# Encoder block on one core: eight chunk pairs of the down projection as block products with weight sums made in DRAM

## The chip, the cores and the metric

The kernel runs on one core of one Trainium2 chip. The metric is the device time of one execution in microseconds (us); a comparison takes the median of several runs. The engines are PE (TensorE, matrix products), DVE (VectorE), ACT (ScalarE), POOL (GpSimd) and SP (SyncE, which issues most transfers). A transfer is carried out by the core's 16 DMA engines, whichever engine issued it.

## The reference

One encoder layer over 512 rows of 1024 columns, in float32: three parallel mixers, a gated feed-forward network (FFN) with 2816 hidden columns (22 tiles of 128), a final norm. The change is in the last product of the FFN, the down projection `act @ w_down`; what stands before it only matters for the order of the work.

```python
h = rms_norm(x, g);  z = h @ W_in                       # gates, latents, streams, memory queries
y = W_out( sum_b sigmoid(g_b) * (o_b @ W_branch_b) )    # attention, mLSTM, attention into memory
x = x + y
x = x + (silu(h2 @ w_gate) * (h2 @ w_up)) @ w_down      # h2 = rms_norm(x); 2816 hidden columns
out = rms_norm(x, g_final)
```

## The kernel before

Each float32 operand is split into a high and a low part, and a product of two 128-row tiles is three matmuls (`mm3`, L104 to L106: high by high, then the two mixed ones). `wload` loads a weight tile of 128x1024 (512 KB) from DRAM into `raw` (SP's queue, L94) and splits it: ACT makes `w_hi` (L85), DVE `w_lo` (L86). `raw` has two buffers and `w_hi`/`w_lo` three.

The code is written against a framework in which tiles have names, pools and buffer counts. A scheduler orders the instructions of each engine by their dependences and priorities; the written order is not the order on the chip. Each engine, SP and POOL among them, runs its own instructions strictly in order, so that an issue which waits holds all issues behind it on the same engine.

At the start SP loads the memory rows, the input and small constants, four tiles of `w_kt` (keys of the memory attention) and then the tiles of `w_zt`, the combined input projection. The z tiles are consumed by PE one after the other, some 6 us each, with attention work in between. POOL makes constants, norm roots, later a `memset` and small stores to `a_dr`.

The FFN uses 2x2 block products with seven multiplications for 19 of its 22 tiles. Its results `u` (tile f) go to `early` (f under 6, kept in SBUF as high and low parts) or to DRAM (`act_dr`, L951). The FFN's `th` and `u` are two-buffer tiles of the pool `fs`, which is released at its end; later pools lie on the same memory.

The down projection is `projection(...)` with `w_fd[half, c]`: two halves of 512 output columns, 11 chunk pairs c of two 128-row tiles each, four row tiles t. In the first half every chunk's activations are read back from `act_dr` and split (`act_load`), and 24 matmuls of 512 columns follow per chunk (4 row tiles, 2 tiles, 3 matmuls). In the second half row tile 3 is computed as two pieces of 256 columns, and the last three chunks are held in `wd_t` so that the row tiles finish one after the other. Then comes `add_part` (L877), the norm and the stores of the output.

Of the kernel before, what the change touches and what calls it, by code (L numbers as in the profile page):

```python
# [60 lines left out]
def block_kernel(ctx, tc, x, mem, pos, inv, g_mix, mem_g, g_ffn, g_final, g_q, g_kv, gate_bias,  # L61
# [966 lines left out]
    act_hi = fin.tile([P, NF - EARLY, S], F32R, name="act_hi")
    act_lo = fin.tile([P, NF - EARLY, S], F32R, name="act_lo")

    def act_side(c):
        if 2 * c < EARLY:
            return early[0], early[1], 2 * c
        return act_hi, act_lo, 2 * c - EARLY

    def act_load(c):
        for f in (2 * c, 2 * c + 1):
            if f >= EARLY:
                a = acte.tile([P, S], F32, name="act", tag="act", bufs=2)
                nc.sync.dma_start(out=a, in_=act_dr[f - EARLY])  # L1040
                split(act_hi[:, f - EARLY], act_lo[:, f - EARLY], a, scale=-0.5)
# [7 lines left out]
    def hold_down(lead):  # L1049
        return [wload(w_fd[1, c], into=wd_t[c - lead]) for c in range(lead, NF // 2)]  # L1050

    def gain_low(t):
        nc.gpsimd.tensor_tensor(out=xg[t][:, :H], in0=x2[t][:, :H], in1=gfin_b[:, :H], op=ALU.mult)

    def store(t, r):
# [1 line left out]
        A.activation(xg[t][:, :H], xg[t][:, :H], AF.Copy, scale=r)
        nc.scalar.dma_start(out=out[rows, :H], in_=xg[t][:, :H])
        n = H // 2 if t == NT - 1 else H
        for c0 in range(H, D, n):  # L1060
            cols = slice(c0, c0 + n)
# [86 lines left out]
```

## Time and profile before

| | us |
|---|---|
| median of three runs | 926.97 |
| lowest, highest | 925.7, 928.73 |
| the profiled execution | 925.3 |
| its span in the profile | 923.4 |
| PE busy | 905.1 |
| DVE busy | 636.1 |
| ACT busy | 509.2 |
| POOL busy | 85.2 |

The span is what the profiler saw of one execution; 1.9 us of that execution lie outside it. Busy times are sums over the whole span. Matmuls are pipelined: the time from one start to the next is the pace, and a row's mean of one is longer than it. DMA share is the mean busy share of the 16 DMA engines, and GB/s is what they moved.

### The profile page before, as it was taken

Reading aid. Unit: us, or ns where it says so; the run is one execution under the profiler, and the core shown is the slowest. Engines: PE = TensorE matmul, PEld = TensorE weight load, DVE = VectorE, ACT = ScalarE, POOL = GpSimd, SP = SyncE. Lnnn points to the kernel's source line nnn. Section 1 sums busy time; section 2 is a strip of 40 time slices with the busy share of each in tenths; the row PEclk is TensorE's granted clock in tenths of the full one; section 3 lists DMA queues with packets and bytes.
Section 4 is the critical chain, followed back from the end, with each engine's and each line's share of the span. In section 5 each row is a group of like instructions: output and inputs, shape, how many; then the busy total and the mean of one; then the engine's idle time right before and its main releaser. Section 6 shows DMA issues by size and latency. Waiting matters only on the chain.

```text
span 923.4 us, 13931 instructions
## 1 busy us (share of the span) xinstructions
PE 905.1 (98%) x5282; PEld 787.7 (85%) x5282; DVE 636.1 (69%) x1088; ACT 509.2 (55%) x896; POOL 85.2 (9%) x139
## 2 busy tenths in 40 slices
PE   7998999999999999999999999999999999999997
PEld 5987787878888788888888879999999999988886
DVE  5768968888684856677553855989898988354323
ACT  8565676686653456677574445545454545244222
POOL 2001002121111101001000500000000000000200
PEclk9999999999999999999999999999999999999999
DMA  7421244434432122121224250423434431365322
GB/s 274 161 75 47 77 133 125 157 121 140 140 111 92 50 86 83 40 87 60 78 69 160 90 191 17 160 93 125 149 115 127 159 115 69 105 225 162 106 76 91
DMA packets 36675, 104.82 MB, mean 114 GB/s; under 512 B 5169, under 2 KB 7537, under 8 KB 36609
## 3 DMA queue, kind: packets, MB, share of 16 engines
q1 hardware_dynamic: 34560, 99.65, 32.4%
q0 software_dynamic: 1184, 3.24, 1.0%
q10 hardware_dynamic: 864, 1.06, 0.3%
q8 instruction: 41, 0.67, 0.3%
q14 instruction: 26, 0.21, 0.1%
HBM read 97.55 MB, written 6.37 MB: 113 GB/s over the span
## 4 chain that ended last, share of the span: by engine, by line
PE 90%; DVE 4%; DMA 2%; ACT 1%; issue 1%; POOL 0%; POOLq 0%; DVEq 0%; SPq 0%; ACTq 0%
PE pg L104 17%; PE pg L106 17%; PE pg L105 17%; PE po L104 7%; PE po L106 7%; PE po L105 7%; PE psc L104 2%; PE psc L105 2%; PE psc L106 2%; PE ptp L818 2%; DVE w_lo L86 1%; PE ppv L588 1%; PE ppv L587 1%; DMA raw<-w_out_d 1%; PE ppv L586 1%
## 5 line engine op out<-in xcount | busy, mean ns | idle before, releaser
L86 DVE TENSOR_TENSOR w_lo<-raw,w_hi 128x1024 fp32r<-128x1024 f32 (+3 forms) x112 | 126.0, 1127 | 92.4 <-ACT w_hi L85 90.7
L104 PE MATMUL pg<-h_hi,w_hi 128*128 128x512 f32 (+1 forms) x476 | 175.2, 369 | 0.8 <-DVE q_lo L89 0.6
L105 PE MATMUL pg<-h_lo,w_hi 128*128 128x512 f32 (+1 forms) x476 | 175.6, 369 | 0.0
L106 PE MATMUL pg<-h_hi,w_lo 128*128 128x512 f32 (+1 forms) x476 | 175.1, 368 | 0.3 <-DVE w_lo L86 0.3
L85 ACT ACTIVATE w_hi<-raw 128x1024 fp32r<-128x1024 f32 (+3 forms) x112 | 107.0, 958 | 104.4 <-PE pg L105 57.2
L104 PEld LDWEIGHTS pg<-h_hi,w_hi 128*128 128x128 f32 x476 | 89.6, 188 | 15.4 <-DVE q_lo L89 0.8
L106 PEld LDWEIGHTS pg<-h_hi,w_lo 128*128 128x128 f32 x476 | 89.5, 188 | 14.8 <-DVE w_lo L86 0.7
L105 PEld LDWEIGHTS pg<-h_lo,w_hi 128*128 128x128 f32 x476 | 89.5, 188 | 13.7
L571 ACT ACTIVATE e<-e,ccol 128x512 f32<-128x512 f32 (+3 forms) x64 | 32.3, 554 | 28.2 <-DMA e<-a_dr 27.6
L1073 DVE TENSOR_REDUCE nm<-psc 128x1 f32<-128x512 f32 (+1 forms) x48 | 27.7, 596 | 19.9 <-PE psc L106 19.5
L576 DVE TENSOR_TENSOR e<-e,psc 128x512 f32<-128x512 f32 (+3 forms) x64 | 29.1, 482 | 17.5 <-POOL e L574 14.6
L1076 ACT ACTIVATE pn<-psc,nm 128x512 f32<-128x512 f32 (+1 forms) x48 | 29.4, 614 | 17.6 <-DVE nm L1073 17.6
L85 ACT ACTIVATE w_hi<-rawab 128x1024 fp32r<-128x1024 f32 x19 | 20.1, 1059 | 29.0 <-PE pg L105 17.4
L574 POOL TENSOR_SCALAR_AFFINE_SELECT e<-e 128x128 f32<-128x128 f32 x64 | 24.0, 384 | 121.5 <-ACT e L571 110.2
L104 PE MATMUL po<-h_hi,w_hi 128*128 128x256 f32 (+1 forms) x116 | 33.8, 291 | 1.4 <-ACT w_hi L85 1.4
L86 DVE TENSOR_TENSOR w_lo<-rawab,w_hi 128x1024 fp32r<-128x1024 f32 x19 | 23.2, 1222 | 16.1 <-ACT w_hi L85 16.0
L1079 ACT ACTIVATE pn<-pn,rs 128x512 f32<-128x512 f32 (+1 forms) x48 | 29.8, 651 | 7.7 <-DVE rs L1078 7.5
L105 PE MATMUL po<-h_lo,w_hi 128*128 128x256 f32 (+1 forms) x116 | 33.7, 290 | 0.0
L106 PE MATMUL po<-h_hi,w_lo 128*128 128x256 f32 (+1 forms) x116 | 33.6, 290 | 0.0
L86 DVE TENSOR_TENSOR s_lo<-e,s_hi 128x640 fp32r<-128x640 f32 x32 | 26.1, 825 | 4.3 <-ACT s_hi L85 2.6
L105 PE MATMUL po<-w_lo,act_hi 128*128 128x512 f32 (+1 forms) x74 | 27.4, 375 | 0.0
L85 ACT ACTIVATE w_hi<-s 128x1024 fp32r<-128x1024 f32 x19 | 20.1, 1059 | 12.9 <-PE pg L105 9.9
(511 smaller groups left out, 2565.3 us busy)
## 6 DMA issues: line engine op xcount, KB each, us to landing
raw<-w_zt_d SPq DMA_DIRECT2D x46, 512.0 KB, 3.4
raw<-w_fd_d SPq DMA_DIRECT2D x22, 512.0 KB, 3.4
e<-a_dr SPq DMA_DIRECT2D x32, 320.0 KB, 3.4
rawab<-w_fg_d SPq DMA_DIRECT2D x19, 512.0 KB, 3.8
rawab<-w_fu_d SPq DMA_DIRECT2D x19, 512.0 KB, 4.7
raw<-w_br_d SPq DMA_DIRECT2D x12, 512.0 KB, 3.5
raw<-w_out_d SPq DMA_DIRECT2D x8, 512.0 KB, 3.6
act_dr<-u SPq DMA_DIRECT2D x16, 256.0 KB, 3.9
```

What stands on the lines that cost most here:

```text
L85: A.activation(hi, src, AF.Copy)
L86: V.tensor_tensor(out=lo, in0=src, in1=hi, op=ALU.subtract)
L104: mm(ps, wh, ah, start=start and i == 0, stop=False, skip_group_check=more)
L105: mm(ps, wh, al, start=False, stop=False, skip_group_check=more)
L106: mm(ps, wl, ah, start=False, stop=stop and i == n - 1, skip_group_check=more)
L571: A.activation(e[:, c0:c0 + n], e[:, c0:c0 + n], AF.Exp, bias=ccol[:, j, d, row:row + 1])
L574: nc.gpsimd.affine_select(out=dg, in_=dg, pattern=[[sgn, P]], compare_op=ALU.is_ge, fill=0.0, base=0, channel_multiplier=-sgn)
L576: V.tensor_tensor(out=e[:, c0:c0 + n], in0=e[:, c0:c0 + n], in1=sc[:, t0:t0 + n], op=ALU.mult)
L818: nc.tensor.transpose(tp[:, c * 256 + q * P:c * 256 + (q + 1) * P], pn[q][:, (kt + c) * P:(kt + c + 1) * P], ident)
L1073: nc.vector.tensor_reduce(out=nm, in_=sc, axis=AX.X, op=ALU.max, negate=True)
L1076: nc.scalar.activation(pn, sc, AF.Exp, bias=nm, accum_out=sm)
L1079: nc.scalar.activation(pn, pn, AF.Copy, scale=rs)
```

## The change

Chunks 0 to 2 (the early tiles, C0 = 3) stay plain products. Chunks 3 to 10 (NC = 8) are computed as 2x2 blocks with seven products instead of eight. The blocks are: rows 0 to 255 and 256 to 511 of the activations, two tiles of the hidden columns per chunk, and two halves of the output columns. The three phases have two, three and two of the products per chunk; each uses some differences of activation blocks (`acts`, `lhs`) and some sums of weight blocks. The products accumulate in PSUM over the chunks, and `onto` adds or subtracts a finished bank to or from `x2`.

The sums of weight blocks (`t13`, `t24`) do not depend on the input of the layer but on `w_fd` alone. They are made in DRAM by `down_sums()`: SP copies a block from DRAM to DRAM (L843, L844, L851, L857 of the new code, 1 MiB each), and POOL issues transfers that add another block onto the copy (L847 2 MiB, L854 and L860 1 MiB; `accum_op=ALU.add`). Everything is done for two groups of four chunks. `beside` interleaves these steps with the units of the latent attention. `weights` takes its `raw` buffers from two pools in turn, `stage` and `fin`. At the very end the first half's weights of the plain chunks are loaded a second time (`ws`).

The diff, cut to its core:

```diff
+    t13, t24 = ([dram.tile([4, P, 2, 512], F32, name=f"{n}_{g}") for g in range(2)] for n in ("t13", "t24"))
...
+        def down_sums():
+            groups = range(2)
+            low, high = ([w_fd[u, C0 + 4 * g:C0 + 4 * g + 4] for g in groups] for u in range(2))
+            for g in groups:
+                nc.sync.dma_start(out=t13[g][:, :, 0], in_=low[g][:, :, 0:512])
+                nc.sync.dma_start(out=t13[g][:, :, 1], in_=high[g][:, :, 512:1024])
+                yield
+            for g in groups:
+                nc.gpsimd.dma_start(out=t13[g], in_=high[g][:, :, 0:512].unsqueeze(2).to_broadcast([4, P, 2, 512]),
+                                    accum_op=ALU.add)
+                yield
+            for g in groups:
+                nc.sync.dma_start(out=t24[g][:, :, 0], in_=t13[g][:, :, 0])
+                yield
+            for g in groups:
+                nc.gpsimd.dma_start(out=t24[g][:, :, 0], in_=high[g][:, :, 512:1024], accum_op=ALU.add)
+                yield
+            for g in groups:
+                nc.sync.dma_start(out=t24[g][:, :, 1], in_=t24[g][:, :, 0])
+                yield
+            for g in groups:
+                nc.gpsimd.dma_start(out=t24[g][:, :, 1], in_=low[g][:, :, 512:1024], accum_op=ALU.add)
+                yield
...
-        run(mla_units(oa_hi, oa_lo), fill, 0.9)
+        run(beside(mla_units(oa_hi, oa_lo), down_sums()), fill, 0.9)
...
+    def acts(c):
+        ab = (acte if c == 0 else fin).tile([P, 2, S], F32, name="ab", tag="ab", bufs=1 if c == 0 else 3)
+        for i in range(2):
+            nc.sync.dma_start(out=ab[:, i], in_=act_dr[2 * c + i])
...
+        d = fin.tile([P, 5, HS], F32, name="d", tag="d", bufs=NC)
+        V.tensor_tensor(out=d[:, 0], in0=a22, in1=a21, op=ALU.subtract)
+        V.tensor_tensor(out=d[:, 1], in0=a21, in1=a11, op=ALU.subtract)
+        V.tensor_tensor(out=d[:, 2], in0=d[:, 0], in1=a11, op=ALU.add)
+        V.tensor_tensor(out=d[:, 3], in0=a12, in1=d[:, 2], op=ALU.subtract)
+        nc.sync.dma_start(out=d[:, 4], in_=act_dr[2 * c + 1][:, HS:])
...
+        raw = (stage if raws[0] % 2 else fin).tile([P, 1024], F32, name="raw", tag="raw", bufs=2)[:, :n]
...
-    projection(((po,) * 4, (pg, pg, pt), (pt, po)),
-               w_fd, NF // 2, 3, act_side, hold_down, gain_low, store, last, act_load)
+    for c in range(C0):
+        w = weights(w_fd[0, c])
+        for t in range(2):
+            plain(py[t], t, c, w, c == 0, False)
+    for c in range(NC):
+        held[c] = acts(c)
+        w = weights(w_fd[0, C0 + c])
+        a = lhs(held[c][0][:, :, :HS], 2, "a2", -0.5)
+        block(px, a, 0, w, 0, c == 0, c == NC - 1)
+        block(py, a, 1, w, 512, False, c == NC - 1)
...
+    for c in range(NC):
+        w13 = weights(t13[g][i].rearrange("p i c -> p (i c)"))
+        s = lhs(held[c][1][:, 0:3], 3, "a3", 0.5)
+        block(pw, s, 0, w13, 0, c == 0, c == NC - 1)
+        block(pz, s, 1, w13, 512, c == 0, c == NC - 1)
+        w2 = weights(t24[g][i, :, 0])
+        block(px, s, 2, w2, 0, False, c == NC - 1)
...
+    for c in range(NC):
+        w = weights(w_fd[1, C0 + c][:, 512:1024], t24[g][i, :, 1])
+        a = lhs(held[c][1][:, 3:5], 2, "a2", -0.5)
+        block(pw, a, 0, w, 0, False, False)
+        block(pz, a, 1, w, 512, False, False)
```

SP's order at the start, before: behind the small constants come the loads of `w_kt` and `w_zt`, and nothing else.

```order
L265 DMA gh_94<-g_head_d 128x4
L265 DMA gq_t<-g_q_d 128x3
L265 DMA gkv_t<-g_kv_d 128x2
L94 DMA raw<-w_kt_d 128x1024 x4
L94 DMA raw<-w_zt_d 128x1024 x7
L94 DMA raw<-w_qk_d 128x256
```

Seven `w_zt` loads follow each other without anything between them; each waits for its `raw` buffer alone.

SP's order at the same place, after. `t_0_72` and `t_1_73` are the two groups of `t13`, `t_0_74` and `t_1_75` those of `t24`.

```order
L843 DMA t_0_72<-w_fd_d 512x512
L97 DMA raw<-w_kt_d 128x1024
L844 DMA t_0_72<-w_fd_d 512x512
L843 DMA t_1_73<-w_fd_d 512x512
L97 DMA raw<-w_kt_d 128x1024
L844 DMA t_1_73<-w_fd_d 512x512
L97 DMA raw<-w_kt_d 128x1024 x2
L97 DMA raw<-w_zt_d 128x1024
L851 DMA t_0_74<-t_0_72 512x512
L97 DMA raw<-w_zt_d 128x1024
L851 DMA t_1_75<-t_1_73 512x512
L97 DMA raw<-w_zt_d 128x1024 x3
L857 DMA t_0_74<-t_0_74 512x512
```

Six copies now stand ahead of the third `w_zt` load (the third to the fifth are the row with x3). Each L851 copy waits for the accumulating transfer of its group on POOL. Two more copies (L857, which wait for the L854 transfers) stand ahead of the sixth and the seventh `w_zt` load.

POOL's order behind the roots of the first norm, before:

```order
L115 TENSOR_TENSOR n_r<-n_v,mhalf 128x1 x6
L433 MEMSET t_633 32x512
L453 DMA a_dr<-brel 8x512
L453 DMA a_dr<-brel 8x384
L453 DMA a_dr<-brel 8x256
```

One `memset` and the first stores to `a_dr` follow. The same place after:

```order
L118 TENSOR_TENSOR n_r<-n_v,mhalf 128x1 x6
L847 DMA t_0_72<-w_fd_d 1024x1x512
L847 DMA t_1_73<-w_fd_d 1024x1x512
L436 MEMSET t_637 32x512
L854 DMA t_0_74<-w_fd_d 512x512
L854 DMA t_1_75<-w_fd_d 512x512
L860 DMA t_0_74<-w_fd_d 512x512
L860 DMA t_1_75<-w_fd_d 512x512
L456 DMA a_dr<-brel 8x512
```

The six accumulating transfers have come in between; each waits for the copies into its tile.

PE's order at the end of the FFN, before (with buffer numbers; `po_8600` is the FFN's last bank, `po_8684` to `po_8687` are the banks of the first half):

```order
L105 MATMUL po_8600<-h2t4l_5903,a22_hi_8520 128x256
L106 MATMUL po_8600<-h2t4h_5902,a22_lo_8521 128x256
L105 MATMUL po_8684<-w_lo_8751,early_h_5888 128x512
L106 MATMUL po_8684<-w_hi_8750,early_l_5889 128x512
L104 MATMUL po_8684<-w_hi_8750,early_h_5888 128x512
...
L104 MATMUL po_8687<-w_hi_8690,early_h_5888 128x512
...
L104 MATMUL po_8684<-w_hi_8788,act_hi_8667 128x512
```

Here 33 plain matmuls on `early` tiles stand between the FFN's last product and the first matmul on `act_hi`, and 39 of them stand ahead of that last product. After (`po_8618` is the FFN's last bank, `po_8702` and `po_8703` are `py`, `pg_8700` and `pg_8701` are `px`):

```order
L108 MATMUL po_8618<-h2t4l_5921,a22_hi_8538 128x256
L109 MATMUL po_8618<-h2t4h_5920,a22_lo_8539 128x256
L107 MATMUL po_8702<-w_hi_8724,early_h_5906 128x512
L107 MATMUL po_8703<-w_hi_8724,early_h_5906 128x512
L108 MATMUL po_8702<-w_lo_8725,early_h_5906 128x512
L109 MATMUL po_8702<-w_hi_8724,early_l_5907 128x512
L107 MATMUL po_8702<-w_hi_8724,early_h_5906 128x512
...
L107 MATMUL po_8702<-w_hi_8742,early_h_5906 128x512
L107 MATMUL po_8703<-w_hi_8742,early_h_5906 128x512
L107 MATMUL pg_8700<-w_hi_8769,a2h_8773 128x512
L107 MATMUL pg_8701<-w_hi_8769,a2h_8773 128x512
```

Of the plain matmuls of this phase 36 are left, and 12 of them stand ahead of the last product. The first weights behind it, `w_hi_8724`, are split from a `raw` buffer of the pool `fin`, which lies on the memory of the FFN's `th`; the `d` tiles lie on that of `u`.

## Rows read from the trace of the kernel before

**Rows 1.** The page's first line, busy times (us, share of the span, instructions) and chain that ended last.

```profile
span 923.4 us, 13931 instructions
PE 905.1 (98%) x5282; PEld 787.7 (85%) x5282; DVE 636.1 (69%) x1088; ACT 509.2 (55%) x896; POOL 85.2 (9%) x139
PE 90%; DVE 4%; DMA 2%; ACT 1%; issue 1%; POOL 0%; POOLq 0%; DVEq 0%; SPq 0%; ACTq 0%
```

**Rows 2.** Windows: start:end, length, busy us (count) by engine, PEclk, DMA share, GB/s.

```profile
0.00:10.00 10.00, 4.62 (x17) 3.19 (x17) 2.49 (x9) 5.43 (x11) 4.64 (x17) 1.00 0.80 283
10.00:20.00 10.00, 9.94 (x36) 7.83 (x37) 8.32 (x18) 10.00 (x18) 1.65 (x3) 1.00 0.96 343
20.00:30.00 10.00, 10.00 (x75) 9.27 (x74) 6.99 (x11) 7.92 (x12) 0.55 (x1) 1.00 0.39 121
```

**Rows 3.** Timeline of SP's queue: start, us, engine, line, operation, tiles, count.

```profile
15.08 9.80 SPq L94 DMA_DIRECT2D raw<-w_kt_d  x4
28.46 2.99 SPq L94 DMA_DIRECT2D raw<-w_zt_d  x2
34.34 3.02 SPq L94 DMA_DIRECT2D raw<-w_zt_d  x2
```

**Rows 4.** Timeline of PE at 12, 49 and 67 us.

```profile
12.37 0.63 PE L105 MATMUL psc<-w_lo,mt_hi 128*128 128x512 f32 x1
12.79 0.63 PE L106 MATMUL psc<-w_hi,mt_lo 128*128 128x512 f32 x1
14.30 0.39 PE L105 MATMUL psc<-w_lo,mt_hi 128*128 128x512 f32 x1
14.53 0.39 PE L106 MATMUL psc<-w_hi,mt_lo 128*128 128x512 f32 x1
48.99 0.39 PE L104 MATMUL ppv<-h_hi,w_hi 128*128 128x512 f32 x1
67.57 0.40 PE L105 MATMUL pg<-h_lo,w_hi 128*128 128x512 f32 x1
```

**Rows 5.** The page's DMA issues: tile, queue, count, KB each, us to landing.

```profile
raw<-w_zt_d SPq DMA_DIRECT2D x46, 512.0 KB, 3.4
```

**Rows 6.** Timeline of ACT: the splits that start consecutive chunks of the down projection.

```profile
828.81 1.06 ACT L85 ACTIVATE w_hi<-raw 128x1024 fp32r<-128x1024 f32 x1 [1.51 <-PE po L106]
834.25 1.06 ACT L85 ACTIVATE w_hi<-raw 128x1024 fp32r<-128x1024 f32 x1 [1.86 <-PE po L106]
867.07 1.06 ACT L85 ACTIVATE w_hi<-raw 128x1024 fp32r<-128x1024 f32 x1 [4.48 <-PE po L106]
872.61 1.06 ACT L85 ACTIVATE w_hi<-raw 128x1024 fp32r<-128x1024 f32 x1 [4.48 <-PE po L106]
```

**Rows 7.** Timeline of POOL: the first stores of `a_dr`.

```profile
73.54 1.31 POOL L453 DMA_DIRECT2D a_dr<-brel  x2 [29.55 <-DVE rs L1078]
```

**Rows 8.** Timeline of all engines where the FFN ends; releaser of idle time in brackets.

```profile
804.66 0.28 PE L106 MATMUL po<-h2t4h,a_lo 128*128 128x256 f32 x1
805.45 0.69 DVE L1013 TENSOR_TENSOR u<-th,u 128x512 f32<-128x512 f32 x1
806.16 0.33 SPq L951 DMA_DIRECT2D act_dr<-u  x1
808.58 1.15 ACT L88 ACTIVATE act_hi<-act 128x512 fp32r<-128x512 f32 x2 [4.64 <-DMA act_dr<-u]
```

**Rows 9.** Timeline of DVE: operations of 256, 512 and 1024 columns in a row.

```profile
750.36 0.42 DVE L994 SCALAR_TENSOR_TENSOR th<-th,g 128x256 f32<-128x256 f32 x1
750.70 0.69 DVE L1013 TENSOR_TENSOR u<-th,u 128x512 f32<-128x512 f32 x1
751.30 1.22 DVE L151 TENSOR_TENSOR s<-rawab 128x1024 f32<-128x1024 f32 x1
752.43 1.22 DVE L86 TENSOR_TENSOR s_lo<-rawab,s_hi 128x1024 fp32r<-128x1024 f32 x1
```

**Rows 10.** Timeline of DVE: the addition behind the last matmul.

```profile
917.21 0.42 DVE L877 TENSOR_TENSOR x<-po,x 128x256 f32<-128x256 f32 x1 [0.58 <-PE po L106]
```

More of the change, by code (lines that the diff above doesn't have):

```diff
@@ L38 @@
 EARLY = 6
+C0 = EARLY // 2
 NEG = -1.0e30
@@ L832, in mla_units, with beside @@
                             yield
+        def down_sums():
[21 more added lines that the diff above has]
+                yield
+        def beside(main, steps):
+            for _ in main:
+                next(steps, None)
+                yield
+            for _ in steps:
+                pass
         run(latent_units(), fill, 0.0)
@@ L1027, in block_kernel @@
     fin = ctx.enter_context(tc.tile_pool(name="fin", bufs=1))
[L1028 to L1041, printed above, removed]
     last = tc.alloc_tile_pool(name="last", bufs=1, side="right")
-    wd_t = [[last.tile([P, 1024], F32R, name=f"wd{c}{i}") for i in range(2)] for c in range(3)]
+    wd_t = [[last.tile([P, 1024], F32R, name=f"wd{c}{i}") for i in range(2)] for c in range(C0)]
     xg = [last.tile([P, D], F32, name=f"xg{t}") for t in range(NT)]
@@ L1047, in block_kernel @@
     bcast_rows(gfin_b, g_final)
[L1049 to L1055, printed above, removed]
-        rows = slice(t * P, (t + 1) * P)
[L1057 to L1061, printed above, removed]
+    NC = NF // 2 - C0
@@ new lines, in lhs, with weights @@
+    def lhs(src, n, tag, scale):
+        hi, lo = (fin.tile([P, n, HS], F32R, name=f"{tag}{i}", tag=f"{tag}{i}", bufs=2) for i in "hl")
+        split(hi, lo, src, scale=scale)
+        return hi, lo
+    raws = [0]
+    def weights(*srcs):
+        raws[0] += 1
+        n = 512 * sum(2 if src.shape[-1] == 1024 else 1 for src in srcs)
+        raw = (stage if raws[0] % 2 else fin).tile([P, 1024], F32, name="raw", tag="raw", bufs=2)[:, :n]
+        o = 0
+        for src in srcs:
+            w = src.shape[-1]
+            nc.sync.dma_start(out=raw[:, o:o + w], in_=src)
+            o += w
+        return wload(None, n=n, raw=raw)
@@ new lines, in block, with plain @@
+    def block(ps, a, i, w, o, first, last):
+        for t in range(2):
+            ts = slice(t * P, (t + 1) * P)
+            mm3(ps[t], [(a[0][:, i, ts], a[1][:, i, ts], w[0][:, o:o + 512], w[1][:, o:o + 512])],
+                start=first, stop=last, more=True)
+    def plain(ps, t, c, w, first, last, cols=slice(0, H)):
+        ts = slice(t * P, (t + 1) * P)
+        mm3(ps, [(early[0][:, 2 * c + k, ts], early[1][:, 2 * c + k, ts], w[0][:, k * H:(k + 1) * H][:, cols],
+                  w[1][:, k * H:(k + 1) * H][:, cols]) for k in range(2)], start=first, stop=last, more=True)
@@ new lines, in onto, with squares, gain @@
+    def onto(ps, t, c0, op=ALU.add, n=H):
+        xs = x2[t][:, c0:c0 + n]
+        V.tensor_tensor(out=xs, in0=xs, in1=ps, op=op)
+    def squares(t, c0, base_v, n=H):
+        junk = last.tile([P, H], F32, name="junk", tag="junk", bufs=2)[:, :n]
+        ss = keep.tile([P, 1], F32, name="ssx", tag="ssx", bufs=2 * NT)
+        A.activation(junk, x2[t][:, c0:c0 + n], AF.Square, accum_out=ss)
+        return partial(ss, base_v)
+    def gain(t, c0):
+        nc.gpsimd.tensor_tensor(out=xg[t][:, c0:c0 + H], in0=x2[t][:, c0:c0 + H], in1=gfin_b[:, c0:c0 + H], op=ALU.mult)
@@ L1062, in store @@
+    def store(t, v, c0, n):
+        r = keep.tile([P, 1], F32, name="f_r", tag="f_r", bufs=2)
+        nc.gpsimd.tensor_tensor(out=r, in0=v, in1=mhalf[:, :1], op=ALU.pow)
+        rows = slice(t * P, (t + 1) * P)
+        done = slice(c0, c0 + H)
+        A.activation(xg[t][:, done], xg[t][:, done], AF.Copy, scale=r)
+        nc.scalar.dma_start(out=out[rows, done], in_=xg[t][:, done])
+        for c1 in range(H - c0, D - c0, n):
+            cols = slice(c1, c1 + n)
             V.scalar_tensor_tensor(out=xg[t][:, cols], in0=x2[t][:, cols], scalar=r, in1=gfin_b[:, cols], op0=ALU.mult, op1=ALU.mult)
@@ new lines, in block_kernel @@
+    for t in range(2):
+        onto(px[t], t, 0)
+        onto(py[t], t, 0)
+        vs[t] = squares(t, 0, EPS)
+        gain(t, 0)
+    pz, pw = [bank(pt) for _ in range(2)], [bank(po) for _ in range(2)]
+    for c in range(NC):
+        g, i = divmod(c, 4)
+        w13 = weights(t13[g][i].rearrange("p i c -> p (i c)"))
[4 more added lines that the diff above has]
+        block(px, s, 2, w2, 0, False, c == NC - 1)
@@ new lines, in block_kernel @@
+    for t in range(2):
+        onto(pw[t], 2 + t, H)
+        onto(pz[t], 2 + t, H, ALU.subtract)
+    py = [bank(po) for _ in range(2)]
+    for c in range(C0):
+        w = wload(w_fd[1, c], into=wd_t[c])
+        for t in range(2):
+            plain(py[t], 2 + t, c, w, c == 0, c == C0 - 1)
+    for t in range(2):
+        onto(px[t], 2 + t, H, ALU.subtract)
+        onto(py[t], 2 + t, H)
+        vs[2 + t] = squares(2 + t, H, EPS)
+        gain(2 + t, H)
+    for t in range(2):
+        onto(px[t], t, H, ALU.subtract)
+        onto(px[t], 2 + t, 0)
@@ new lines, in block_kernel @@
+    for c in range(NC):
+        g, i = divmod(c, 4)
+        w = weights(w_fd[1, C0 + c][:, 512:1024], t24[g][i, :, 1])
+        a = lhs(held[c][1][:, 3:5], 2, "a2", -0.5)
+        block(pw, a, 0, w, 0, False, False)
+        block(pz, a, 1, w, 512, False, False)
+    for t in range(2):
+        for c in range(C0):
+            plain(pw[t], t, c, wd_t[c], False, c == C0 - 1)
+        onto(pw[t], t, H)
+        store(t, squares(t, H, vs[t]), 0, H)
+    ws = [weights(w_fd[0, c]) for c in range(C0)]
@@ L1067, in block_kernel @@
+    for t in range(2):
+        v = vs[2 + t]
+        n = H // (1 + t)
+        for c0 in range(0, H, n):
+            cols = slice(c0, c0 + n)
+            for c in range(C0):
+                plain(pz[t][:, cols], 2 + t, c, ws[c], False, c == C0 - 1, cols)
+            onto(pz[t][:, cols], 2 + t, c0, n=n)
+            v = squares(2 + t, c0, v, n)
+        store(2 + t, v, H, n)
     for pool in (last, pt, po, pg):
```

6 lines of the change are left out of this document (added).

## Prediction

> **What bounds the kernel now.** I read the page's totals first. PE is busy 905.1 of 923.4 us, and PE has 90% of the chain that ended last; DVE has 4%, DMA 2% [rows 1]. So a matmul that is taken away is worth its time where PE does not wait, and any wait put in front of PE is added, since there is no idle time later that could win it back. Then I read three stretches, because the change touches the program at two places far apart: the first 50 us, where the new sums are issued, and the end from 800 us, where the down projection lies.
>
> The windows show that the first 20 us are a transfer stage: 283 GB/s in the first 10 us, 343 GB/s with the DMA engines 0.96 busy in the second [rows 2]. From 20 us PE is 10.00 of 10.00 busy and the DMA share falls to 0.39. SyncE (SP) issues the loads in program order: four `w_kt` tiles from 15.08 us, then the `w_zt` tiles (call them z0, z1, ...), two from 28.46 and two from 34.34, so z2, the third, goes out at 34.34 [rows 3]. PE begins on z2 (the product into `ppv`) at 48.99, and on z5 (whose first record here is its second matmul) at 67.57 [rows 4]. These are deadlines.
>
> **The start: the sums.** `down_sums()` depends on nothing, and the order shows that it has come to the front, ahead of and among these loads. Per group there are two copies of 1 MiB into `t13`, one accumulating transfer of 2 MiB, a copy of 1 MiB from `t13` to `t24`, an accumulate of 1 MiB, a copy of 1 MiB, an accumulate of 1 MiB; two groups. The copies are on SP's queue, and the L851 copy waits there for the accumulate of its group. z1 is queued behind the first L851, z2 behind the second. So z2 cannot be issued before 6 MiB of copies are asked for and 4 MiB of accumulates have landed.
>
> What must have moved before z2 is in: the 5 MiB that the start loads already, seven tiles of 0.5 MiB (`w_kt` 0 to 3, z0 to z2), 6 MiB of copies, 4 MiB of accumulates.
> - 1 MiB is 1.049 MB, at 343 GB/s [rows 2] 3.06 us. The first 5 MiB (5.24 MB): 2.83 MB in the first 10 us, the other 2.41 MB take 7.0, so 17.0 us. Seven tiles: 3.5 × 3.06 = 10.7.
> - A copy inside DRAM has no row. It reads and writes DRAM where a load only reads it: between once and twice the load's price, 3.06 to 6.1 per MiB; no row is nearer to one end, and I take the middle, 4.6: 6 × 4.6 = 27.5.
> - An accumulate has no row either. It reads two sources and writes one: from the load's price (once) to three times it, 3.06 to 9.2; I take twice, 6.1: 4 × 6.1 = 24.5.
> - From the last byte to PE: landing is 3.4 us from issue [rows 5], of which 1.5 is the transfer itself, so 1.9; the split by ACT is 1.06 [rows 6]. Together 3.0.
>
> 17.0 + 10.7 + 27.5 + 24.5 + 3.0 = 82.7, against 48.99 wanted: **33.7 us late**. With both at the load's price, 17.0 + 10.7 + 18.4 + 12.2 + 3.0 = 61.3, 12.3 late. With both at their high ends, 17.0 + 10.7 + 36.7 + 36.7 + 3.0 = 104.1, 55 late. A gain is excluded at this place: nothing that PE does here is taken away. The earlier tiles are late too, but delays here are not added: each only moves what follows, and the last one, z2's, is the largest.
>
> The Trainium skill ("DMA: Bandwidth & Descriptors", section "Latency and other measured facts") gives copies between DRAM tensors 207 to 214 GB/s at full rate, an estimate of about 5 us per MiB and 30 for the 6 MiB; with it the sum would be about 2 us later. No run here shows it yet. It speaks against this change in a second place: "Collectives: The Full Stack", Part 3, "Why ReduceScatter is half of AllGather", says that an add done by the DMA is slow because it needs two source reads, and so half the copy's rate. With twice my copy price for the accumulates (9.2 per MiB) the sum would be 12.2 later. My value is the lower one; the other is inside my upper bound.
>
> Behind z2 the second half of the sums holds SP again: z5 is behind the first L857 copy, which waits for the first L854 accumulate. From the arrival of z2's last byte (79.7), z3 to z5 4.6, one or two accumulates of 6.1 and one copy of 4.6 end at 95 to 101, plus 3.0 is 98 to 104; wanted at 67.57 + 33.7 = 101.3. So about on time, 0 to 3 more. GpSimd's accumulates stand before its `a_dr` stores, which ran at 73.54 [rows 7] and are wanted by then plus the delay, 107: hidden while the second accumulates have landed by then.
>
> One more cost of the wait: at 12.4 us the matmuls followed each other in 0.42, at 14.3 in 0.23 [rows 4]. If PE falls back to the slow pace in the gap, the next tile of 24 matmuls costs up to 24 × 0.2 = 4.8 more. I count it in the upper bound only.
>
> **The down projection.** Before: 462 matmuls of 512 columns and 132 of 256 (the last row tile's second half). After: the 8 pairs take 8 × 42 = 336 in place of 384, 144 plain ones stay, and 36 are of 256: 462 and 36. So 96 short ones go. A chunk of 24 full ones is 834.25 − 828.81 = 5.44 us, 0.227 each; a chunk of 18 full and 12 short 872.61 − 867.07 = 5.54 [rows 6]; a short one is (5.54 − 18 × 0.227)/12 = 0.122. **Gain 96 × 0.122 = 11.7 us**, if PE stays full.
>
> It does not stay full at the join with the FFN. Before, 39 plain matmuls stand ahead of the last FFN product and 33 behind it, so that the last `u` (805.45), its store (806.16) and the first activations read back (808.58) [rows 8] are covered. After, only 12 stand ahead, so the FFN's last product ends 27 × 0.227 = 6.1 earlier, at 798.7; behind it come 24 plain and 96 block matmuls, 120 × 0.227 = 27.2, to 825.9 if nothing waits. But the new `raw` and `d` tiles lie on the memory of the FFN's `th` and `u`, free at 800.0 and, for `u`, after its store, 2.4 later (808.58 − 806.16) at 802.4. From there DVE must do, for this phase, 31 operations of 128x256, 8 of 512 columns, 2 of 768 and 10 of 1024: at paces of 0.34, 0.60 and 1.13 [rows 9] (768 between, 0.87) 10.5 + 4.8 + 1.7 + 11.3 = 28.3, to 830.7. With 1 to 2 us for arrivals and the last block's 12 matmuls (2.7) the phase ends near 835: **9.1 us lost**. Low bound 5.8: the first weights alone are read from 800.0 and ready after 3.4 + 1.06, at 804.5 against 798.7. High bound 13, if loads and DVE alternate. Phases 2 and 3 are PE's: 18 matmuls of 0.227 are 4.1 us per chunk against some 2.7 of DVE, 12 are 2.7 against 1.8; 0 to 2 lost. The tail behind the last matmul, from 917.21 to the end [rows 10], is the same work. The down projection is worth 11.7 − 9.1 = **2.6**, between −2 and 6.
>
> The scheduler also moves work in the middle (attention, mLSTM): no row prices this, 0 ± 2.
>
> **The sum.** The profiled execution took 925.3, its span 923.4 and 1.9 around it. 925.3 + 33.7 − 2.6 = 956.4. The median of the three runs, 926.97, is 1.7 above that execution: 958.1, so **958**.
>
> **Rivals.**
> 1. *The sums are hidden, and it is not slower.* From 20 us the DMA engines are 0.39 busy [rows 2]; if copies and accumulates fit there, z2 comes in time, and the time is 927 − 2.6 = 924, or 915 if DVE keeps up too. The point where it decides: 13.5 MiB (14.2 MB) between 17.0 and 46.0, 488 GB/s counting each byte once. No window shows more than 343. By the down projection's whole gain of 11.7 it is no slower as long as z2 is under 12 us late, which is the low bound. [...]
> 2. *Both at the load's price*: 12.3 late, 925.3 + 12.3 − 2.6 + 1.7 = 937.
> 3. *Both at the high prices*, or the accumulates still slower: 925.3 + 55 − 2.6 + 1.7 = 979, with the slow pace and z5 late up to 987.
>
> **Chances.** My forecast 0.47, rival 1 0.16 (its times lie on both sides of 924.2: 0.10 under it, 0.06 within 0.3%), rival 2 0.19, rival 3 0.18. This kernel's measurement can tell 0.3%, 2.8 us. Rival 2 with a down projection at its best end gives some 0.02 more within. So faster 0.10, within 0.3% 0.08, slower 0.82. The range leaves out rival 1 and a few hundredths above rival 3: 931 to 988.
>
> **What would show it.** Right: in the profile after, SP issues z1 and z2 after the accumulates landed, PE is idle before z0 to z2 with `raw<-w_zt` as releaser, some 30 us in all in the first 90, and the DMA share is near 1 from 20 to 75 us. At the join PE stops after the last FFN product for some 6 us, DVE is nearly full in phase 1, and phases 2 and 3 have PE full. Wrong: PE full between 20 and 60 us (rival 1); the accumulates of 2 MiB landing within 7 us of each other, or over 18 (rivals 2 and 3); a PE without idle time at 799 to 835, which makes the gain 11.7; or a wait in the middle that no row here shows.

## The result and the profile after

The changed kernel takes 964.87 us (median of 4 runs, 964.27 to 968.11) against 927.85 for the kernel before in the same comparison: a ratio of 1.0406, with a 95% interval of 1.0371 to 1.0441. The profiled execution has a span of 963.2 us, 39.8 longer than before.

The page of the changed kernel, its span, busy times and the chain that ended last:

```profile
span 963.2 us, 13963 instructions
PE 911.1 (95%) x5186; PEld 785.1 (82%) x5186; DVE 680.8 (71%) x1159; ACT 530.2 (55%) x923; POOL 94.1 (10%) x145
PE 75%; DMA 11%; DVE 7%; ACT 4%; issue 2%; POOL 1%; SPq 0%; POOLq 0%; DVEq 0%; ACTq 0%
```

Against [rows 1], PE is busy 6.0 us longer although it has 96 matmuls fewer, its share falls from 98% to 95%, and DMA holds 11% of the chain where it had 2%. So the time went into PE waiting for transfers, and into slower matmuls after such waits.

SP's queue, at the place of [rows 3] (start, us, engine, line, operation, tiles, count):

```profile
50.51 0.48 SPq L851 DMA_DIRECT2D t<-t  x1
51.09 0.56 SPq L97 DMA_DIRECT2D raw<-w_zt_d  x1
64.42 0.48 SPq L851 DMA_DIRECT2D t<-t  x1
65.00 0.57 SPq L97 DMA_DIRECT2D raw<-w_zt_d  x1
```

z1 goes out at 51.09 and z2 at 65.00, each right behind an L851 copy. Before, they went out at 31.13 (inside the pair that begins at 28.46) and 34.34. GpSimd's queue tells what the L851 copies waited for (releaser of the idle time in brackets):

```profile
27.91 2.07 POOL L847 DMA_DIRECT2D t<-w_fd_d  x1 [6.47 <-DMA t<-w_fd_d]
37.46 1.84 POOL L847 DMA_DIRECT2D t<-w_fd_d  x1 [7.48 <-DMA raw<-w_kt_d]
63.21 1.03 POOL L854 DMA_DIRECT2D t<-w_fd_d  x1 [7.14 <-DMA t<-t]
```

The two accumulates of 2 MiB are issued at 27.91 and 37.46. By the two L851 copies, which go out as soon as they have landed, they land 22.6 and 27.0 us later, at 50.5 and 64.4. The third row is to be noted: the accumulate of the second half (L854) is issued at 63.21, ahead of z2's load.

Windows over the same stretch (busy us of PE, PEld, DVE, ACT and POOL, PEclk, DMA share, GB/s):

```profile
20.00:30.00 10.00, 7.36 (x37) 6.24 (x36) 4.48 (x7) 5.14 (x8) 2.62 (x2) 0.86 1.02 339
50.00:60.00 10.00, 9.20 (x41) 7.61 (x39) 1.89 (x3) 0.63 (x2) 0.52 (x1) 0.78 1.10 245
60.00:64.00 4.00, 0.34 (x2) 0.00 (x0) 0.00 (x0) 0.00 (x0) 0.79 (x1) 1.00 0.55 185
64.00:68.00 4.00, 1.88 (x4) 1.07 (x5) 1.83 (x2) 1.54 (x2) 0.24 (x1) 0.58 0.79 88
79.00:84.00 5.00, 4.82 (x11) 3.33 (x12) 3.76 (x7) 3.56 (x9) 0.00 (x0) 0.50 0.98 127
10.00:79.10 69.10, 49.26 (x231) 40.26 (x231) 26.24 (x43) 26.74 (x42) 8.68 (x9) 0.87 0.99 267
```

The DMA engines are full to 60 us, but while accumulates run they move 245 GB/s where loads moved 343 [rows 2]. From 60 to 68 the share is 0.55 and 0.79: SP stands still until 64.42, and too little is asked for. PE is busy 0.34 of the first 4 us there. The last row holds the whole stretch from 10 us to the start of z2: PE is idle for 19.8 of 69.1 us, and busy for 49.3 at a granted clock of 0.87 with work that took the kernel before 38.9 of the 39.0 us from 10 to 49.

PE at z2 and at the tile behind it, as in [rows 4]:

```profile
79.14 0.80 PE L107 MATMUL ppv<-h_hi,w_hi 128*128 128x512 f32 x1 [3.86 <-ACT w_hi L88]
81.42 0.63 PE L108 MATMUL ppv<-h_lo,w_hi 128*128 128x512 f32 x1
87.75 0.40 PE L107 MATMUL pg<-h_hi,w_hi 128*128 128x512 f32 x1
```

z2 begins at 79.14 instead of 48.99, 30.2 us late. Behind the gap the matmuls first follow each other in 0.60 and then in 0.43 us, about as at 12.4 us in [rows 4], and only after twelve of them in 0.23. The granted clock is 0.50 from 79 to 84 us (the last window above), which is the lower of the two levels (1.2 GHz of 2.4). The next tile begins at 87.75, where the kernel before was at 55.16: 32.6 late.

The first product of the FFN's blocks, before and after, gives the delay at 600 us:

```profile
615.50 0.28 PE L104 MATMUL pg<-h_hi,s_hi 128*128 128x256 f32 x1
```

```profile
654.60 0.28 PE L107 MATMUL pg<-h_hi,s_hi 128*128 128x256 f32 x1
194.75 0.58 PE L589 MATMUL ppv<-s_hi,vh 128*66 128x384 f32 x1 [3.47 <-ACT s_hi L88]
```

654.60 − 615.50 = 39.1: another 6.5 us were lost between 88 and 654. The second row of the second view is the largest single place, a wait of 3.47 us for a weight of the mLSTM that ACT makes from `e`, a tile that is loaded from `a_dr`. From 88 to 200 us PE is idle for 6.6 us, against 3.6 over the same stretch of the kernel before (55.2 to 167).

Last, the join with the down projection, as in [rows 8], and the first 30 us behind it:

```profile
837.65 0.28 PE L109 MATMUL po<-h2t4h,a_lo 128*128 128x256 f32 x1
846.45 1.22 PE L107 MATMUL po<-w_hi,early_h 128*128 128x512 f32 x2 [8.53 <-ACT w_hi L88]
839.14 0.32 SPq L986 DMA_DIRECT2D act_dr<-u  x1
841.60 0.33 SPq L1100 DMA_DIRECT2D raw<-w_fd_d  x1
846.00:876.00 30.00, 29.51 (x122) 23.85 (x123) 28.74 (x50) 17.62 (x22) 0.00 (x0) 0.94 0.92 332
```

PE ends the FFN at 837.65 and stands still for 8.53 us. The first weights behind it are asked for at 841.60, 2.5 us after the store of the last `u` went out (839.14); by the trace the landing of that store is what this issue waited for. From 846 on PE is full (29.51 of 30), with DVE at 28.74. From the FFN's first block product to the end the kernel before took 923.4 − 615.5 = 307.9, and this one 963.2 − 654.6 = 308.6.

So the 39.8 us between the two profiled executions are: 30.2 at z2, 2.4 by the slow pace after it, 6.5 in the middle, 0.7 at the end.

### The profile page after: what moved, and what is told of

Same layout as the page of the kernel before. It is cut to its first block, busy times and chain, and to the rows that moved or that the text cites. A ratio compares the mean times of both kernels' runs of the same rounds, so it can differ in the third digit from the quotient of the medians.

```text
span 963.2 us, 13963 instructions
## 1 busy us (share of the span) xinstructions
PE 911.1 (95%) x5186; PEld 785.1 (82%) x5186; DVE 680.8 (71%) x1159; ACT 530.2 (55%) x923; POOL 94.1 (10%) x145
## 4 chain that ended last, share of the span: by engine, by line
PE 75%; DMA 11%; DVE 7%; ACT 4%; issue 2%; POOL 1%; SPq 0%; POOLq 0%; DVEq 0%; ACTq 0%
PE pg L107 14%; PE pg L108 14%; PE pg L109 14%; PE po L107 6%; PE po L108 6%; PE po L109 6%; DMA t<-w_fd_d 3%; DMA raw<-w_zt_d 2%; DMA e<-a_dr 2%; DMA raw<-w_kt_d 2%; DVE w_lo L89 2%; PE ptp L821 1%; PE psc L107 1%; PE psc L108 1%; PE psc L109 1%
## 5 line engine op out<-in xcount | busy, mean ns | idle before, releaser
L89 DVE TENSOR_TENSOR w_lo<-raw,w_hi 128x1024 fp32r<-128x1024 f32 (+3 forms) x131 | 146.4, 1122 | 96.8 <-ACT w_hi L88 95.3
L88 ACT ACTIVATE w_hi<-raw 128x1024 fp32r<-128x1024 f32 (+3 forms) x131 | 123.2, 944 | 115.5 <-PE pg L108 45.0
L107 PE MATMUL pg<-h_hi,w_hi 128*128 128x512 f32 (+1 forms) x476 | 177.2, 372 | 6.4 <-ACT w_hi L88 5.7
L89 DVE TENSOR_TENSOR w_lo<-rawab,w_hi 128x1024 fp32r<-128x1024 f32 x19 | 23.3, 1224 | 16.0 <-ACT w_hi L88 15.9
L108 PE MATMUL po<-h_lo,w_hi 128*128 128x256 f32 (+1 forms) x116 | 33.7, 290 | 0.0
L89 DVE TENSOR_TENSOR s_lo<-e,s_hi 128x640 fp32r<-128x640 f32 x32 | 26.1, 821 | 4.5 <-ACT s_hi L88 4.4
L88 ACT ACTIVATE w_hi<-s 128x1024 fp32r<-128x1024 f32 x19 | 20.1, 1060 | 12.8 <-PE pg L108 9.9
L88 ACT ACTIVATE s_hi<-e 128x640 fp32r<-128x640 f32 x32 | 22.7, 726 | 8.0 <-DVE e L579 7.9
```

## The experiments

All ratios are to the kernel before, measured beside it on the same chip (its medians there were 928 to 929).

**Without the sums (e1_no_sums).**

```diff
-        run(beside(mla_units(oa_hi, oa_lo), down_sums()), fill, 0.9)
+        run(mla_units(oa_hi, oa_lo), fill, 0.9)
...
-        w13 = weights(t13[g][i].rearrange("p i c -> p (i c)"))
+        w13 = weights(w_fd[1, C0 + c])
```

> The changed kernel without down_sums: the sums of weight blocks are left out, and phases 2 and 3 load plain blocks of w_down of the same sizes in their place (so the result is not the reference's). Theory A, the sums at the start cost the time (z2 begins 30 us late, with the slow pace after it 33): the time falls by 33 to 40, to 925 to 932, and the first 100 us are those of the kernel before. Theory B, the rest of the change (order in the middle, the join, the three phases) carries a large part: the time stays above 940. The down projection alone, by the prediction, is worth 2.6, 925; by the trace of the changed kernel about 0 to -1, 927 to 929.

930.98 us, ratio 1.0033 (1.0009 to 1.0057). PE at z2, at the FFN's first block product, and behind the FFN:

```profile
49.76 0.39 PE L106 MATMUL ppv<-h_hi,w_hi 128*128 128x512 f32 x1
618.47 0.28 PE L106 MATMUL pg<-h_hi,s_hi 128*128 128x256 f32 x1
810.36 1.22 PE L106 MATMUL po<-w_hi,early_h 128*128 128x512 f32 x2 [8.56 <-ACT w_hi L87]
```

The start is the old one (49.76), and theory A's number is met. The 8.56 us at the join are still there. So what is left of the change without its sums is not worth 2.6 us; over the whole kernel it costs 0.8 to 5.3. In this execution the FFN's first block product is 3.0 late (618.47 against 615.50), of which 0.8 is there at z2.

**The sums alone (e2_sums_only).**

```diff
-        run(mla_units(oa_hi, oa_lo), fill, 0.9)
+        run(beside(mla_units(oa_hi, oa_lo), down_sums()), fill, 0.9)
```

> The kernel before with down_sums added and nothing else; nobody reads the sums. Theory A: the whole loss is here, 960 to 967, with z2 beginning at some 79 us. Theory B: under 945.

965.22 us, ratio 1.0416 (1.0389 to 1.0444): the whole loss. PE at the same two places:

```profile
79.61 0.79 PE L106 MATMUL ppv<-h_hi,w_hi 128*128 128x512 f32 x1 [3.58 <-ACT w_hi L87]
654.56 0.28 PE L106 MATMUL pg<-h_hi,s_hi 128*128 128x256 f32 x1
```

z2 and the FFN start where they do in the changed kernel, to 0.5 us. Between the two places it loses 8.4 us more (39.1 − 30.6), the slow pace behind z2 included, against 8.9 in the changed kernel. So the loss in the middle comes with the sums too: the down projection of this kernel is the old one. But e1's execution lost 2.2 us over the same stretch without any sums, so a part of it need not be theirs.

**What an accumulate costs beside a copy (e4_no_add).**

```diff
-                nc.gpsimd.dma_start(out=t24[g][:, :, 0], in_=high[g][:, :, 512:1024], accum_op=ALU.add)
+                nc.gpsimd.dma_start(out=t24[g][:, :, 0], in_=high[g][:, :, 512:1024])
```

and the same for the other two lines.

> The changed kernel with every accumulating transfer made a plain copy of the same blocks, on the same queues and with the same waits (so the sums are not made, and the result is not the reference's). By the prediction's prices, 6.1 against 4.6 per MiB, z2 is 6 us earlier and the time 957 to 960. By the prices of e9 alone, 5.0 against some 3.8, 4 to 5 earlier, 959 to 961. Rival, an accumulate costs twice a copy: 15 to 20 earlier, 945 to 950. If the time is set by the waits of SP on completions and not by bytes: unchanged, 963 to 967.

947.57 us, ratio 1.0215 (1.0185 to 1.0244): 17.3 less than the changed kernel, in the middle of the rival's range of times. PE at z2, and two windows in which copies from both queues and loads run, those with the most and the least moved from 28 to 56 us:

```profile
67.49 0.40 PE L107 MATMUL ppv<-h_hi,w_hi 128*128 128x512 f32 x1
28.00:32.00 4.00, 3.36 (x22) 3.12 (x21) 1.42 (x4) 1.04 (x3) 1.41 (x1) 0.78 1.04 388
48.00:52.00 4.00, 2.38 (x11) 2.17 (x12) 1.55 (x2) 1.88 (x2) 0.00 (x0) 0.78 0.98 318
```

With copies in place of the accumulates the engines move 318 to 388 GB/s at a share of about 1, about as much as they did with loads [rows 2]. So a copy costs about 3.0 us per MiB (1.049 MB at 353, the middle), and the adding is what made the stretch slow. z2 comes 11.7 us earlier than in the changed kernel, less than the 15 to 20 of the rival whose time was met; the other 5.6 us are gained behind z2.

**The prices by themselves (e9_price).**

```diff
+    for _ in range(2):
+        nc.gpsimd.dma_start(out=half, in_=low[:, :, 0:512])
+    for _ in range(2):
+        nc.gpsimd.dma_start(out=half, in_=high[:, :, 512:1024], accum_op=ALU.add)
...
+    for _ in range(2):
+        nc.gpsimd.dma_start(out=t, in_=high[:, :, 0:512].unsqueeze(2).to_broadcast([4, P, 2, 512]), accum_op=ALU.add)
```

> Nothing of the block is computed: each kind of transfer of the sums runs alone, one after the other on one DRAM tile, twice each: a copy of 1 MiB by SP, the same by GpSimd, an accumulate of 1 MiB, a copy of 1 MiB within the tile, an accumulate of 2 MiB, a load of 2 MiB into SBUF. From issue to landing, by the prediction's prices (with its 1.9 us of latency): load 2 MiB 8.0, copy 1 MiB 6.5, accumulate 1 MiB 8.0 and 2 MiB 14.1. Rival, an accumulate costs twice a copy: 11 and 20. Rival, all bytes cost about the same once they flow (the windows of the changed kernel show 245 to 290 GB/s in every mix): about 4 per MiB for copies and accumulates, 6 and 10 with latency.

The issues, each of which waits for the one before it (L81 copies by GpSimd, L83 accumulates of 1 MiB, L85 copies by SP, L87 accumulates of 2 MiB, L89 loads of 2 MiB):

```profile
19.97 0.65 POOL L81 DMA_DIRECT2D t<-w_fd_d  x1 [5.67 <-DMA t<-w_fd_d]
26.45 1.06 POOL L83 DMA_DIRECT2D t<-w_fd_d  x1 [5.83 <-DMA t<-w_fd_d]
37.29 1.04 POOL L83 DMA_DIRECT2D t<-w_fd_d  x1 [9.77 <-DMA t<-w_fd_d]
47.42 6.42 SPq L85 DMA_DIRECT2D t<-t  x2
59.76 1.82 POOL L87 DMA_DIRECT2D t<-w_fd_d  x1 [21.43 <-DMA t<-t]
74.45 1.81 POOL L87 DMA_DIRECT2D t<-w_fd_d  x1 [12.88 <-DMA t<-w_fd_d]
88.77 8.31 SPq L89 DMA_DIRECT2D big<-t  x2
```

The one execution took 115.13 us. From start to start: a copy of 1 MiB 6.5 (19.97 to 26.45), an accumulate of 1 MiB 10.8 and 10.1, one of 2 MiB 14.7 and 14.3; a load of 2 MiB lands in 8.0. The prediction's prices come out for the load, the copy and the accumulate of 2 MiB (8.0, 6.5, 14.1), not for the accumulate of 1 MiB (8.0); for the rival "twice a copy" it is the other way round (11 holds, 20 does not). Five windows (DMA share and GB/s at the end), two inside an accumulate of 1 MiB, one inside one of 2 MiB, one inside a copy and one inside a load:

```profile
41.00:43.00 2.00, 0.00 (x0) 0.00 (x0) 1.00 1.01 105
43.00:45.00 2.00, 0.00 (x0) 0.00 (x0) 1.00 1.03 163
67.00:69.00 2.00, 0.00 (x0) 0.00 (x0) 1.00 1.13 208
50.00:52.00 2.00, 0.00 (x0) 0.00 (x0) 1.00 0.97 328
92.00:94.00 2.00, 0.00 (x0) 0.00 (x0) 1.00 0.98 395
```

At full share the accumulate of 2 MiB, which reads each source row twice, moves 208 GB/s, 5.0 us per MiB; that of 1 MiB some 134, 7.8 per MiB. "All bytes cost the same" is refuted. A copy alone moves 328, 3.2 us per MiB, 1.2 times the price of the load (395). The Trainium skill's "Collectives: The Full Stack" (Part 3, "Why ReduceScatter is half of AllGather") has the transfers of a reduction at half the rate of plain copies, because an add needs two source reads. Against 328 the accumulates here are 1.6 and 2.4 times slower, so the trace agrees that an add costs more, by an amount on either side of that 2; the reason for it was not tried. The Trainium skill's "DMA: Bandwidth & Descriptors" ("Latency and other measured facts") gives, per direction, 207 to 214 GB/s for copies between DRAM tensors of another layout at large pitches. The copies of e9 show more (328), and the measurement decides here.

**The sums on GpSimd's queue (e3_sums_on_pool).**

```diff
+            def add(**kw):
+                with tc.issue_after(sums_after[0]):
+                    nc.gpsimd.dma_start(**kw)
...
-                nc.sync.dma_start(out=t13[g][:, :, 0], in_=low[g][:, :, 0:512])
+                add(out=t13[g][:, :, 0], in_=low[g][:, :, 0:512])
```

and so for all seven lines (fourteen transfers, as there are two groups); `sums_after` is the last root of the first norm.

> The changed kernel with all sixteen MiB of sums on GpSimd's queue, behind the last root of the first norm (some 21 us); SP's queue holds only the loads again, in the old order. Theory A1, the loads are late because SP stands still until the accumulates have landed: the loads now share the DMA engines with the sums instead of waiting for them, z2 is late by less than 10 us, and the time is 930 to 942. Theory A2, the DMA engines have to move the bytes of the sums first wherever they are issued: z2 is late by 25 us or more and the time stays at 955 to 967.

959.85 us, ratio 1.0359 (1.0330 to 1.0388). The time is A2's, but the mechanism is neither. PE at z2, two issues of GpSimd, what DVE waited for, and PE's longest wait (its row stands at the end of the wait):

```profile
61.82 0.40 PE L107 MATMUL ppv<-h_hi,w_hi 128*128 128x512 f32 x1
100.12 1.03 POOL L845 DMA_DIRECT2D t<-w_fd_d  x1 [2.99 <-DMA t<-t]
100.76 1.44 POOL L459 DMA_DIRECT2D a_dr<-brel  x2
113.92 1.00 DVE L455 TENSOR_TENSOR_SCAN brel<-t,t 32x256 f32<-32x256 f32 x2 [13.83 <-DMA a_dr<-brel]
116.40 0.51 PE L465 MATMUL ptp<-ident,crow 32*128 32x32 f32 x2 [11.72 <-DVE crow L457]
```

With SP free, z2 begins at 61.82, 12.8 late instead of 30.2: taking the sums off SP's queue gave back 17 us there. The sums also begin some 6 us later here, so not all of the 17 need be SP's standing still. But now GpSimd stands still. Its first `a_dr` stores go out at 100.76 (73.54 in [rows 7]), behind the last accumulate at 100.12. DVE, which works on with what they wrote, waits for them to 113.92, 13 us after the issue, where such stores landed in about 2 us in the kernel before; then PE has waited 11.72 us for `crow`. The wait was moved to another queue and taken there, once in the order of the issues and once more behind the bytes of the accumulates.

**The sums beside the FFN (e5_sums_late).**

```diff
-            nc.gpsimd.tensor_tensor(out=r, in0=v, in1=mhalf[:, :1], op=ALU.pow)
+            sums_after[:] = [nc.gpsimd.tensor_tensor(out=r, in0=v, in1=mhalf[:, :1], op=ALU.pow).ins]
```

and `down_sums()` as in e3, behind the last of these roots.

> The changed kernel with the same sums on GpSimd's queue, but behind the last root of the second norm, so that they run beside the FFN (from some 570 us), where GpSimd has nothing to do and the DMA engines are about a third busy. Theory A: the start is that of the kernel before; if the FFN's own loads are not late, the time is that of the kernel without sums, 925 to 929. Rival: the sums slow the FFN's weight loads, which come every 11 us in pairs of 1 MiB in all, and PE waits for them: 935 or more.

945.50 us, ratio 1.0197 (1.0170 to 1.0224): the rival held. PE's two largest waits from 500 to 720 us (engine, tile and line, releaser, us in total, times, longest), and one window:

```profile
PE po L109 <- DVE w_lo L89: 3.8, 2, 3.6
PE pg L107 <- ACT w_hi L88: 2.4, 1, 2.4
640.00:660.00 20.00, 16.43 (x125) 16.23 (x125) 13.67 (x20) 9.52 (x16) 2.72 (x3) 0.91 1.01 249
```

Nothing is queued behind the sums here, on SP or GpSimd, and still they cost 14.5 us over e1: the DMA share is 1.01 at 249 GB/s, the FFN's weights come late, and after each wait the clock is low for a while (0.91 over this window). The trace shows no wait in an issue queue behind the sums, so what they cost here is the time of the DMA engines.

**The sums beside the latent attention (e7_sums_spread).**

```diff
+        def add(mark, **kw):
+            with tc.issue_after(adds[mark]):
+                nc.gpsimd.dma_start(**kw)
...
+            add(1, out=t13[g][:, :, 0], in_=low[g][:, :, 0:512])
```

> The changed kernel with the sums on GpSimd's queue beside the latent attention (some 330 to 500 us), in steps, each behind one of the eight additions that GpSimd makes there anyway; the loads of that stage keep the DMA engines 0.14 to 0.26 busy. Theory, sums cost what they hold up and nothing more: no load is late here, and the time is that of the changed kernel without sums, 929 to 934. Rival, the sums slow the loads wherever they run, as beside the FFN: 938 to 948.

936.60 us, ratio 1.0086 (1.0055 to 1.0117): between the two, 5.6 over e1. `adds` are GpSimd's eight additions. The largest wait in this stage (at its end):

```profile
358.83 0.38 PE L829 MATMUL ppv<-pth,vv 128*128 128x256 f32 x1 [1.66 <-ACT pth L88]
```

The four copies that go out together are issued 21 us before it, and ACT makes this `pth` behind a split that waited 1.49 us for a load of weights. With one other wait it makes 2.4 us; the rest of the 5.6 was not traced. The cheapest of the places tried, but not free.

**Another join (e8b_nosums_join).**

```diff
-        w = weights(w_fd[0, c])
-        for t in range(2):
-            plain(py[t], t, c, w, c == 0, False)
+        w = weights(w_fd[0, c], step=c == 0)
+        with tc.issue_after(last_mm[0]) if c else ExitStack():
+            for t in range(2):
+                plain(py[t], t, c, w, c == 0, False)
```

With `step` 0 a tile stays in the pool `stage`, and the first block chunk's weights do so too; `last_mm` is the FFN's last matmul.

> The kernel without sums (sums left out, plain blocks of w_down read in their place) with another join of FFN and down projection: all weights of the plain chunks and of the first block chunk come from the buffers of stage, which are free before the FFN ends, and the plain products of chunks 1 and 2 stand behind the FFN's last product. Theory M, PE stops there for 8.6 us because those weights wait for the FFN's th and u memory: the stop falls to under 1.5 and the time by 7 to 9, to 921 to 924. Theory D, VectorE's work paces phase 1, as in the prediction's sum: PE waits later in the phase instead, and the time falls by less than 4, 927 to 931.

929.22 us, ratio 1.0007 (0.9992 to 1.0022), 1.8 under e1 (the two intervals overlap). Theory M's 7 to 9 are refuted. Where PE waits now, and what SP and DVE do before it:

```profile
816.72 0.79 PE L108 MATMUL pg<-w_hi,a2h 128*128 128x512 f32 x1 [4.05 <-ACT w_hi L87]
810.38 0.43 SPq L1077 DMA_DIRECT2D raw<-w_fd_d  x1
812.04 0.43 DVE L1057 TENSOR_TENSOR d<-ab 128x256 f32<-128x256 f32 x1 [1.02 <-DMA ab<-act_dr]
```

The stop of 8.6 us is gone, and 4.05 us of waiting stand one chunk later: those weights, in `fin`, went out at 810.38, behind activations. Theory D's number holds, but not its reason: DVE itself waits for activations at 812.04. What is short seems to be neither engine but the loads that start only when the last `u` has been stored (its store goes out at 805.69, the first of these loads at 808.07). The next run tries that.

**One chunk more in the old buffers (e10_nosums_join2).**

```diff
-        w = weights(w_fd[0, C0 + c], step=c > 0)
+        w = weights(w_fd[0, C0 + c], step=c > 1)
```

> As e8b_nosums_join (sums left out, plain blocks read in their place), with the weights of the second block chunk also in a buffer of stage. In e8b the stop moved to that chunk: its weights, loaded into fin's memory behind the activations, came 4 us late, while VectorE itself waited for activations. Theory L, what remains is a burst of loads that cannot start before the last u is stored: the second chunk's weights are there, 2.7 us of products cover more of the burst, and the time falls by 2 to 4 more, to 925 to 927. Theory D, VectorE's work paces the phase: no change, 928 to 931.

926.47 us, ratio 0.9983 (0.9966 to 1.0000), 2.75 under e8b: the number of theory L. The intervals of the two runs overlap a little, so the gain is not quite clear of noise by itself. The longest wait left:

```profile
819.88 1.12 PE L108 MATMUL pg<-w_hi,a2h 128*128 128x512 f32 x2 [2.81 <-ACT w_hi L87]
```

It is one chunk later again and shorter, 2.81 us, as theory L has it.

**Both edits (e8_spread_join and e11_spread2_join2).** The first is e7 with the join of e8b; the second is e7 with the join of e10 and its first copies in two steps, the later steps moved to fit:

```diff
-            add(1, out=t13[g][:, :, 0], in_=low[g][:, :, 0:512])
-            add(1, out=t13[g][:, :, 1], in_=high[g][:, :, 512:1024])
+            add(1 + g, out=t13[g][:, :, 0], in_=low[g][:, :, 0:512])
+            add(1 + g, out=t13[g][:, :, 1], in_=high[g][:, :, 512:1024])
```

> Both edits in one: the sums spread beside the latent attention, and the other join. If both theories hold (sums free there, theory M), 921 to 925, faster than the kernel before; with theory D 927 to 932; if the sums slow the loads 930 or more.

933.34 us, ratio 1.0065 (1.0044 to 1.0085), 4.1 over e8b: the last of the three cases, the sums slow the loads here too.

> The join of e10 with the sums on GpSimd's queue beside the latent attention, the first four copies now in two steps of 2 MiB (in e7 and e8 they went out together at 334 us, and PE then waited some 2 us for weights). Theory, a burst of copies delays the loads of this stage: 2 to 4 faster than e8, that is 1 to 2 over e10, 926 to 930. Rival, the sums cost 4 to 6 here however they are spread: 930 to 934.

929.78 us, ratio 1.0030 (1.0013 to 1.0046), 3.3 over e10, inside the expected 926 to 930, though the sums cost a little more than the 1 to 2 expected. This is the best version that makes the sums, 35 us faster than the changed kernel, and still 0.3% slower than the kernel before. None beat it.

## Why the prediction was right, and where its steps were off

The forecast was 958, the measurement 964.87. The direction, the place and the mechanism were as forecast: z1 and z2 held on SP behind copies that wait for accumulates, PE idle in front of them. e1 and e2 show it from both sides: without the sums the loss is gone, and with nothing but the sums it is all there. Step by step, against the profiled executions (1.7 us lie outside the span after, 1.9 before):

- **z2 33.7 late: measured 30.2.** Near, but by terms that cancel, and so in part by luck. Copies were put at 27.5 and cost, by e4's windows, 6 × 3.0 = 18.0. Accumulates were put at 24.5 and cost, by e9's 208 GB/s, 4 × 5.0 = 20.0. Two things were not in the sum: the L854 accumulate issued ahead of z2's load (7.8 by e9), and the hole at 60 to 68 us, in which SP stands still (4 × 0.45 + 4 × 0.21 = 2.6). 17.0 + 10.7 + 18.0 + 20.0 + 7.8 + 2.6 + 3.0 = 79.1, against 79.14. This split is worked out from rows of other kernels and is not shown directly; with e9's 3.2 for a copy it would be 80.3. The mis-sized step is the choice of the middle for the copies: they cost about what loads cost, 1.2 times by e9, near the end that [rows 2] gave.
- **The accumulate against the copy.** Taken 1.33 to 1, measured 1.6 and 2.4 to 1 (e9). As a price the 6.1 per MiB lies between the 5.0 and the 7.8 measured. The two accumulates of 2 MiB landed 13.9 us apart, between the 7 and the 18 that were to speak for the rivals.
- **PE idle for some 30 us in the first 90: too much.** It is idle for 19.8 us from 10 us to z2; the rest of the 30.2 is work that took 10.3 us longer there, at a granted clock of 0.87.
- **The slow pace, in the upper bound only: 2.4 behind z2.** It came (twelve matmuls at 0.60 to 0.43 instead of 0.23; the next tile is 32.6 late and z2 30.2), and it belonged in the sum, since a gap of this length was forecast.
- **z5 about on time: right.** PE's idle time from 80 to 100 us is 0.04 of 20.
- **The middle, 0 ± 2: measured 6.5.** This is the term with the largest miss, and its cause stays open. From z2 to the FFN, the slow pace included, e2 lost 8.4 with the sums alone and this kernel 8.9; e1 lost 2.2 without them. PE is idle for 4.5 us more in the middle than in the kernel before.
- **The down projection, 2.6 gained: measured 0.7 lost** (308.6 against 307.9), and in e1's execution 1.8 lost (928.2 − 618.5 = 309.7). The 9.1 at the join were nearly right in size: PE stops 8.5 there, and the slow pace takes another 1.8 (0.06 of 30). Phases 2 and 3 have PE full, as forecast (74.00 of the 74 us from 876 to 950). The 11.7 of the matmuls were not measured by themselves; 8.5 + 1.8 − 0.7 leaves 9.6 of them, if nothing else changed. But the mechanism was half wrong. I had the first weights free when `th` was read, and DVE as the pace of the phase. The weights went out only after the store of `u` (841.60), and behind the stop PE is full although DVE is busy 28.74 of 30. e8b and e10 point to the loads behind that store as the limit.

Together: −3.5 at z2, +2.4 pace, +6.5 middle, +3.3 down projection is +8.7 on 956.4, 965.1; the profiled execution took 964.9.

Of the rivals, "the sums are hidden" is refuted even at the places with the emptiest queues: 37 us at the start (e2), 14.5 beside the FFN, 3.3 to 5.6 beside the attention. The sums cannot hide at the start, first because SP's own loads stand behind the waits, and second because the bytes take engine time that the loads need. Rival 2 had the copies nearly right and the accumulates too cheap; rival 3 had both too dear.
